# First keys cast in halves, first queries cast and half copied by ScalarE, one key load on another queue, two more warming matmuls

## The chip, the cores and the metric

The kernel runs on one core of a Trainium2 chip. The metric is the device time of one execution in microseconds (us). The core has a matrix engine (PE, TensorE), a vector engine (DVE, VectorE), a scalar engine (ACT, ScalarE), a general one (POOL, GpSimd) and a sequencer that mostly issues transfers (SP, SyncE). Each engine works through its own list of instructions in order, and semaphores hold an instruction back until what it needs is there. Transfers (DMAs) are issued from the lists of SP, ACT and POOL and run beside the engines.

## What is computed

Grouped-query attention: 8 batches, 512 positions, 32 query heads, 8 key/value heads of 64 elements; four query heads share one key/value head.

```python
def reference(Q, K, V):          # Q (8, 512, 32, 64); K, V (8, 512, 8, 64)
    heads_per_group = 32 // 8
    scale = 1.0 / np.sqrt(64)
    K_expanded = np.repeat(K, heads_per_group, axis=2)
    V_expanded = np.repeat(V, heads_per_group, axis=2)
    ...
    scores = np.einsum('bhqd,bhkd->bhqk', Q, K_expanded) * scale
    weights = np.exp(scores - np.max(scores, axis=-1, keepdims=True))
    weights = weights / (np.sum(weights, axis=-1, keepdims=True) + 1e-10)
    output = np.einsum('bhqk,bhkd->bhqd', weights, V_expanded)
    return output.transpose(0, 2, 1, 3).astype(np.float32)
```

## The kernel before

The work is cut into 64 jobs, one for each batch and key/value head; two neighbouring heads make a unit (`u`, with `g` 0 or 1 in it). A job has four query heads in two pairs. For each pair and each of four blocks of 128 keys, PE multiplies keys by queries (`scores`, L217) for both heads of the pair into a PSUM tile of 128 x 2 x 512 numbers. ACT takes the exponential of most of these tiles (`act_tile`, L233), 128 x 1024 at a time; two or three halves per job are instead computed by DVE and POOL from integer arithmetic (`exp_d`, L243, and the functions after it). PE then multiplies the weights by V with a column of ones beside it (`pv`, L300), and DVE divides by the sums (`norm`, L343). The maximum is not subtracted; a flag computed at the end decides whether a general path has to run instead.

The order of the instructions is written out by hand in `fast_path` and no planner moves anything: what stands earlier in the program comes earlier in its engine's list. The job loop (L446) interleaves one job's scores with the last job's products.

The change is in what stands ahead of the loop (L414 to L443). It has these steps.

- Loads. SP's queue gets the first key head in fp32 (`kf[0]`, by `key_head(0)`) and behind it the second (`kf[1]`, `key_head(1)`); ACT's queue gets the first two query heads in fp32 (`qf`, L418). All others go through POOL's queue, which casts to bf16 on the way: the second pair of the first group (`load_q(0, 2, 4)`), the second group's four heads (`load_q(0, 4, 8)`), and then V and K in pieces. POOL also sets a column of ones in the two V tiles (L425).
- Warming. Four matmuls of 128 x 512 zeros (L438) into a scores tile, which nothing reads.
- Keys. `first_keys(0, ...)` (L151): DVE casts `kf[0]` to bf16 into `twice`, each head's 64 columns written two times side by side (L153); PE transposes the four 128-row blocks (L158) into a PSUM bank; `copy()` is DVE's copy of them to `kt_first` (L159).
- Queries. DVE casts `qf` into `qn[0]` (L442). `trans_q(0, bank[:, 0, :], 0, 1)` (L178) lets PE transpose four blocks (L185), and DVE copies the 512 columns to `qt` (L189).

In the loop's job 0, the first scores tile follows, then the transposes of the second pair (`trans_q(0, bank[:, 1, :], 1, NPAIR)`, L470), the second tile, two score products for DVE in the `d_ps` tile, two more tiles, and then twelve transposes: eight of the next job's queries, and four in `first_keys(1, ...)` (L499), whose cast of `kf[1]` stands there on DVE's list. The scores tiles are taken in turn from two PSUM buffers, so the fourth tile waits until the second exponential has been computed.

POOL loads later units of Q only after a gate (L455) that reads the fourth exponential of job 0.

Of the kernel before, what the change touches and what calls it, by code (L numbers as in the profile page):

```python
# [12 lines left out]
BF16 = mybir.dt.bfloat16  # L13
# [3 lines left out]
I32 = mybir.dt.int32  # L17
ALU = mybir.AluOpType
EXP = mybir.ActivationFunctionType.Exp
AX = mybir.AxisListType  # L20


# [17 lines left out]
@with_exitstack  # L40
def kernel(
    ctx: ExitStack,
    tc: tile.TileContext,
    Q: bass.AP,
    K: bass.AP,
    V: bass.AP,
    out: bass.AP,
):
    nc = tc.nc
    flag_pool = ctx.enter_context(tc.tile_pool(name="flag", bufs=1))  # L50
    flag = flag_pool.tile([1, 1], I32, name="flag")
    with ExitStack() as fast, tc.manual_schedule():
        fast_path(fast, tc, Q, K, V, out, flag)
    good = nc.values_load(flag, min_val=0, max_val=128)
    with tc.If(good < 128):
        general_path(tc, Q, K, V, out)


def fast_path(ctx, tc, Q, K, V, out, flag):
    nc = tc.nc  # L60
    B, S, H, D = Q.shape
    KV = K.shape[2]
    HPG = H // KV
    SC = S // 128
    GP = KV // 2
    NU = B * GP
    NPAIR = HPG // 2
# [5 lines left out]
    const_pool = ctx.enter_context(tc.tile_pool(name="const", bufs=1))  # L73
    qnat_pool = ctx.enter_context(tc.tile_pool(name="qnat", bufs=4))
    knat_pool = ctx.enter_context(tc.tile_pool(name="knat", bufs=2))
    qt_pool = ctx.enter_context(tc.tile_pool(name="qt", bufs=3))
# [11 lines left out]
    ident = const_pool.tile([128, 128], BF16, name="ident")  # L88
# [4 lines left out]
    warm = const_pool.tile([128, S], BF16, name="warm")  # L93
# [4 lines left out]
    kf = [const_pool.tile([128, SC, D], FP32, name=f"kf{g}") for g in range(2)]  # L98
    qf = const_pool.tile([128, SC, 2, D], FP32, name="qf")

    kn, qn, kt, qt = {}, {}, {}, {}

    def load_k(b, lo=0, hi=KV):
        if b not in kn:
# [29 lines left out]
    def d_tile():  # L134
        return d_pool.tile([128, 2, S], FP32, name="d_ps")
# [3 lines left out]
    def first_k(gp, swap, bank):  # L139
# [8 lines left out]
                nc.tensor.transpose(ps[:, sc, :], kn[0][:, sc, h:h + 2, :], ident)  # L148
        return lambda: nc.vector.tensor_copy(out=kt_first[:, gp, swap, :], in_=half_bank)

    def first_keys(g, bank):  # L151
        twice = const_pool.tile([128, SC, 2, D], BF16, name=f"twice{g}")
        nc.vector.tensor_copy(  # L153
            out=twice, in_=kf[g][:, :, None, :].to_broadcast((128, SC, 2, D))
        )
        half_bank = bank.bitcast(BF16)[:, 0:S]
        for sc in range(SC):
            nc.tensor.transpose(half_bank[:, sc * 128:(sc + 1) * 128], twice[:, sc, :, :], ident)  # L158
        return lambda: nc.vector.tensor_copy(out=kt_first[:, 0, g, :], in_=half_bank)  # L159

    def dma_k(b):
# [9 lines left out]
    def apart(this, other):  # L171
        if other is not None:
            tc.declare_no_dep(
                this.ins, other.ins, reason="the two are in different banks of one tile"
            )
        return this

    def trans_q(j, bank, lo=0, hi=NPAIR, other=None):  # L178
        u, g = divmod(j, 2)
        ps = bank.bitcast(BF16).rearrange("p (i sc c) -> p i sc c", i=NPAIR, sc=SC)  # L180
        for i in range(lo, hi):
            for sc in range(SC):
                h = g * HPG + 2 * i
                apart(
                    nc.tensor.transpose(ps[:, i, sc, :], qn[u][:, sc, h:h + 2, :], ident), other  # L185
                )
        if u not in qt:
            qt[u] = qt_pool.tile([128, 2, NPAIR, S], BF16, name="qt")
        return lambda: apart(nc.vector.tensor_copy(  # L189
            out=qt[u][:, g, lo:hi, :], in_=ps[:, lo:hi, :, :].rearrange("p i sc c -> p i (sc c)")  # L190
        ), other)

    def check_v(b, sc):
        n = b * SC + sc
        nc.vector.tensor_reduce(  # L195
            out=okv[:, n:n + 1], in_=vt[b % 2][:, sc, :, 0:D], op=ALU.max, axis=AX.XY,
            apply_absolute_value=True,
# [35 lines left out]
    def act_tile(j, n, spare=None):  # L233
# [3 lines left out]
        for _, _, m in group:  # L237
            scores(j, ps[:, m, :], i, kc, m)
        return nc.scalar.activation(  # L239
            out=jobs[j]["pt"][:, i, kc, lo:, :], in_=ps[:, lo:, :], func=EXP, scale=scale  # L240
        )
# [101 lines left out]
    def norm(j, i):  # L343
        st = jobs[j]
        u, g = divmod(j, 2)
        sums = st["pv"][i]
        if u not in osb:
            osb[u] = osb_pool.tile([128, SC, 2 * HPG, D], FP32, name="o_sb")
        p = j * NPAIR + i
        left = NJOB * NPAIR - p  # L350
        k, n = divmod(p, SPB)
        if left <= NLAST:
            inv = inv_last[:, NLAST - left]
        else:
            if k not in invs:
                invs[k] = inv_pool.tile([128, SPB, 2, SC], FP32, name="inv")
            inv = invs[k][:, n]
        nc.vector.reciprocal(out=inv, in_=sums[:, :, :, D:D + 1])  # L358
        if left == 1:
            last_check()  # L360
        h = g * HPG + 2 * i
        nc.vector.tensor_tensor(  # L362
            out=osb[u][:, :, h:h + 2, :].rearrange("p qc m d -> p m qc d"),
            in0=sums[:, :, :, 0:D],
            in1=inv[:, :, :, None].to_broadcast((128, 2, SC, D)),
            op=ALU.mult,
        )
        if u == NU - 1:
            store(u, h, h + 2)
        elif g == 1 and i == NPAIR - 1:  # L370
            store(u, 0, 2 * HPG)
        if left > NLAST and n == SPB - 1:
            full.append((k, SPB))
        if left == NLAST + 1:
            full.append((k, n + 1))
            check_sums()
            vmax = const_pool.tile([128, 1], FP32, name="vmax")
            nc.vector.tensor_reduce(out=vmax, in_=okv, op=ALU.max, axis=AX.X)
            okmin = const_pool.tile([128, 1], FP32, name="okmin")
            nc.vector.tensor_reduce(out=okmin, in_=ok, op=ALU.min, axis=AX.X)  # L380
            nc.vector.scalar_tensor_tensor(
                out=okall, in0=vmax, scalar=V_HI, in1=okmin, op0=ALU.is_le, op1=ALU.mult
            )
# [24 lines left out]
    def pv_tile():  # L408
        return pv_pool.tile([128, 2, S], FP32, name="pv")

    def s_tile():
        return s_pool.tile([128, 2, S], FP32, name="s_ps")

    def key_head(g):  # L414
        nc.sync.dma_start(out=kf[g], in_=K[0, :, g, :].rearrange("(sc p) d -> p sc d", p=128))

    key_head(0)
    nc.scalar.dma_start(out=qf, in_=Q[0, :, 0:2, :].rearrange("(sc p) h d -> p sc h d", p=128))  # L418
    key_head(1)
    make_identity(nc, ident)  # L420
    load_q(0, 2, 4)
    load_q(0, 4, 8)
# [9 lines left out]
    nc.gpsimd.memset(ok, 1.0)  # L432


    nc.vector.memset(warm, 0.0)
    bank = s_tile()
    for j in range(4):
        nc.tensor.matmul(bank[:, 1, :], warm[:, 0:128], warm, start=True, stop=True)  # L438
    copy = first_keys(0, d_tile()[:, 0, :])
    copy()  # L440
    bank = pv_tile()
    nc.vector.tensor_copy(out=qn[0][:, :, 0:2, :], in_=qf)  # L442
    trans_q(0, bank[:, 0, :], 0, 1)()  # L443


    for j in range(NJOB):  # L446
# [3 lines left out]
        u, g = divmod(j, 2)  # L450
# [39 lines left out]
        if not end:  # L490
            bank = d_tile() if j else pv_tile()
            beside = act_tile(j, 4, bank) if taken(j) > 2 else None

            ahead = (j + 1,) if j < 6 else (7, 8) if j == 6 else (j + 2,)
            for n, to in enumerate(ahead):
                if to < NJOB:
                    reads.append(trans_q(to, bank[:, n, :], other=beside))
            if j == 0:
                reads.append(first_keys(1, bank[:, 1, :]))  # L499
            elif j == 1:  # L500
                reads.append(first_k(1, 1, bank[:, 1, :]))
            elif j > 1 and b == 0 and gp + 1 < GP:
                reads.append(first_k(gp + 1, g, bank[:, 1, :]))
        else:
            pv(j, 0, 0, 16)
# [26 lines left out]
        if end:  # L532
# [3 lines left out]
            norm(j, 1)  # L536
    nc.vector.tensor_reduce(out=flag, in_=ends[0], op=ALU.min, axis=AX.X)


def general_path(tc, Q, K, V, out):  # L540
# [8 lines left out]
    with ExitStack() as ctx:  # L549
# [5 lines left out]
        with tc.For_i(0, B, 1) as b:  # L555
            with tc.For_i(0, KV, 1) as g:
# [14 lines left out]
                with tc.For_i(0, HPG, 1) as i:  # L571
# [13 lines left out]
                    for qc in range(SC):  # L585
                        s_ps = ps.tile([128, S], FP32, name="g_s")
                        nc.tensor.matmul(s_ps, q_t[:, qc, :], k_t, start=True, stop=True)
                        top = sb.tile([128, 1], FP32, name="g_top")
                        nc.vector.tensor_reduce(out=top, in_=s_ps, op=ALU.max, axis=AX.X)
                        less = sb.tile([128, S], FP32, name="g_less")  # L590
# [5 lines left out]
                        total = sb.tile([128, 1], FP32, name="g_sum")  # L596
                        nc.scalar.activation(out=e, in_=less, func=EXP, accum_out=total)
                        inv = sb.tile([128, 1], FP32, name="g_inv")
# [56 lines left out]
```

## Time and profile before

| | |
|---|---|
| time, median of 3 runs | 417.14 us (417.10, 417.14, 418.14) |
| time of the profiled execution | 417.43 us |
| its span, first to last instruction | 415.8 us |
| PE busy | 378.1 us (91%) |
| DVE busy | 342.6 us (82%) |
| ACT busy | 400.6 us (96%) |
| POOL busy | 301.5 us (73%) |
| bytes moved by DMA | 67.20 MB, mean 162 GB/s |

Busy shares are means over the whole span. PE's times are partly modelled, since matmuls are pipelined; when one row holds several instructions ("x4"), its time runs from the first one's start to the last one's end. Where the text gives a "chain of waits", it is followed back from the last instruction of the span or of a stretch of it: at each step to what ended the wait, or to the instruction before on the same engine. A row of the order of time has the start in us, the length in us, the engine, the line, the operation, what is written from what, and how many; in square brackets stands the idle time ahead and what ended it.

### The profile page before, as it was taken

The page shows a single profiled execution, that of the slowest core. Times are in us where ns is not written, and L with a number is a line of the kernel's source. Part 1 is how long each engine was busy: PE and PEld are TensorE (multiplying, and loading weights), DVE is VectorE, ACT ScalarE, POOL GpSimd, SP SyncE. Part 2 cuts the span into 40 slices and gives each one's busy share as a digit, 9 for nine tenths or more (in the row PEclk, how much of TensorE's full clock was granted, in tenths as well). Part 3 has the DMA queues.
Part 4 walks back from the last instruction along what each step waited for, and adds up shares of the span by engine and source line. Part 5 has one row for each costly group of instructions (what it writes and reads, how often), then busy time and mean ns, then how long its engine had stood idle before and what let it go on. Part 6 is the DMA issues. An engine that isn't in the chain of part 4 may idle for free.

```text
span 415.8 us, 13054 instructions
## 1 busy us (share of the span) xinstructions
PE 378.1 (91%) x5681; PEld 233.7 (56%) x5681; DVE 342.6 (82%) x609; ACT 400.6 (96%) x449; POOL 301.5 (73%) x213
## 2 busy tenths in 40 slices
PE   5899999999999999999999999999999999999983
PEld 2555655555655555655655655555655555655652
DVE  3677888888888888988888888888889888898875
ACT  3999999999999999999999999999999999999992
POOL 9677665887678886797776897587876887667550
PEclk9999999999999999999999999999999999999998
DMA  9999976799849997399974999669995899732223
GB/s 136 162 165 188 191 154 153 107 214 187 171 139 205 127 222 160 114 217 130 240 181 94 208 180 215 159 85 219 188 173 151 173 160 213 162 110 102 102 102 107
DMA packets 91966, 67.20 MB, mean 162 GB/s; under 512 B 52097, under 2 KB 75137, under 8 KB 91905
## 3 DMA queue, kind: packets, MB, share of 16 engines
q0 software_dynamic: 55488, 24.91, 51.8%
q1 hardware_dynamic: 35888, 41.16, 36.1%
q8 instruction: 45, 0.74, 0.7%
q10 hardware_dynamic: 528, 0.26, 0.2%
q14 instruction: 17, 0.13, 0.1%
HBM read 50.33 MB, written 33.55 MB: 202 GB/s over the span
## 4 chain that ended last, share of the span: by engine, by line
ACT 84%; PE 10%; DVE 3%; issue 1%; DMA 1%; ACTq 0%; DVEq 0%
ACT pt L239 84%; PE s_ps L221 6%; PE pv L315 3%; DMA kf<-in_K_dram 1%; DVE o_sb L362 1%; DVE pt L284 1%; PE pv L185 1%; PE d_ps L185 1%; DVE qt L189 0%; DVE ok L326 0%; ACTq L239 0%; DVE w L267 0%; DVE f L271 0%; PE d_ps L146 0%; DVE twice L153 0%
## 5 line engine op out<-in xcount | busy, mean ns | idle before, releaser
L239 ACT ACTIVATE pt<-s_ps 128x1024 f16<-128x1024 f32 x420 | 397.4, 1289 | 6.1 <-PE s_ps L221 6.1
L315 PEld LDWEIGHTS <-pt 128*128 128x128 f16 x4096 | 142.1, 98 | 75.7 <-issue 56.1
L315 PE MATMUL pv<-v,pt 128*128 128x65 bf16 x4032 | 178.2, 195 | 1.0 <-DVE o_sb L362 0.5
L267 POOL TENSOR_TENSOR w<-g,f 128x1024 bf16<-128x1024 bf16 (+1 forms) x63 | 161.0, 2555 | 5.2
L221 PE MATMUL s_ps<-qt,kt 64*128 64x512 bf16 x728 | 142.6, 383 | 22.3 <-ACT pt L239 16.3
L263 POOL TENSOR_SCALAR g<-f 128x1024 bf16<-128x1024 int16 (+1 forms) x63 | 77.4, 1229 | 96.6 <-DVE f L271 96.6
L250 DVE TENSOR_SCALAR u<-d_ps 128x1024 int16<-128x1024 f32 (+1 forms) x92 | 96.8, 1052 | 1.1 <-PE d_ps L221 1.1
L362 DVE TENSOR_TENSOR o_sb<-pv,inv 128x512 f32<-128x512 f32 x125 | 86.4, 691 | 4.3
L221 PEld LDWEIGHTS <-kt 64*128 64x128 bf16 x896 | 51.8, 93 | 62.3 <-issue 34.9
L358 DVE RECIPROCAL inv<-pv 128x8 f32<-128x8 f32 x125 | 25.9, 207 | 54.6 <-PE pv L315 54.5
L284 DVE TENSOR_TENSOR pt<-u,w 128x1536 uint16<-128x1536 int16 (+1 forms) x64 | 51.1, 798 | 0.1
L221 PE MATMUL d_ps<-qt,kt 64*128 64x512 bf16 x168 | 43.0, 375 | 0.0
L189 DVE COPY qt<-d_ps 128x1024 bf16<-128x1024 bf16 x62 | 42.3, 684 | 0.0
L185 PEld LDWEIGHTS <-q_nat 128*128 128x128 bf16 x512 | 29.3, 99 | 21.1 <-issue 20.0
L185 PE MATMUL d_ps<-ident,q_nat 128*128 128x128 bf16 x496 | 38.3, 220 | 0.0
L271 DVE TENSOR_SCALAR f<-u 128x1536 int16<-128x1536 int16 (+1 forms) x64 | 30.6, 478 | 0.0
L114 POOL DMA_DIRECT2D v<-in_V_dram x32 | 29.0, 909 | 0.1
L129 POOL DMA_DIRECT2D q_nat<-in_Q_dram x33 | 27.0, 818 | 0.2 <-issue 0.2
L221 PE MATMUL s_ps<-qt,kt_first 64*128 64x512 bf16 x112 | 23.1, 407 | 4.2 <-ACT pt L239 3.0
L239 ACT ACTIVATE pt<-d_ps 128x512 f16<-128x512 f32 x28 | 25.2, 899 | 0.0
L195 DVE TENSOR_REDUCE okv<-v 128x1 f32<-128x512 bf16 x32 | 21.6, 676 | 0.0
L221 PEld LDWEIGHTS <-kt_first 64*128 64x128 bf16 x128 | 7.9, 95 | 11.9 <-issue 8.3
(52 smaller groups left out, 44.5 us busy)
## 6 DMA issues: line engine op xcount, KB each, us to landing
out_dram<-o_sb SPq DMA_DIRECT2D x31, 1024.0 KB, 6.8
q_nat<-in_Q_dram POOLq DMA_DIRECT2D x31, 512.0 KB, 6.2
k_nat<-in_K_dram POOLq DMA_DIRECT2D x7, 512.0 KB, 8.3
v<-in_V_dram POOLq DMA_DIRECT2D x28, 128.0 KB, 7.5
kt<-kt SPq DMA_DIRECT2D x14, 256.0 KB, 4.6
out_dram<-o_sb SPq DMA_DIRECT2D x4, 256.0 KB, 2.4
kt<-k_nat SPq DMA_TRANSPOSE x28, 5.8
v<-in_V_dram POOLq DMA_DIRECT2D x4, 96.0 KB, 8.4
```

The lines of the kernel that those rows point to most:

```text
L114: nc.gpsimd.dma_start(out=vt[b % 2][:, sc, lo:hi, 0:D], in_=V[b, sc * 128:(sc + 1) * 128, lo:hi, :],)
L185: nc.tensor.transpose(ps[:, i, sc, :], qn[u][:, sc, h:h + 2, :], ident), other
L189: return lambda: apart(nc.vector.tensor_copy(out=qt[u][:, g, lo:hi, :], in_=ps[:, lo:hi, :, :].rearrange("p i sc c -> p i (sc c)")), other)
L221: return nc.tensor.matmul(ps, keys[64 * m:64 * m + 64, g if u == 0 else g ^ m, kc * 128:(kc + 1) * 128], qt[u][64 * m:64 * m + 64, g, i, : ...
L239: return nc.scalar.activation(out=jobs[j]["pt"][:, i, kc, lo:, :], in_=ps[:, lo:, :], func=EXP, scale=scale)
L250: return lambda: nc.vector.tensor_scalar(out=st["u"][:, lo:hi, :], in0=ps[:, 0:hi - lo, :], scalar1=A_U, scalar2=B_U, op0=ALU.mult, op1=AL ...
L263: engine.tensor_scalar(out=g, in0=f, scalar1=-EXP_F1, scalar2=EXP_K * 2.0 ** (24 * as_bits), op0=ALU.add, op1=ALU.mult,)
L267: engine.tensor_tensor(out=w, in0=g, in1=f.bitcast(FP16) if as_bits else f, op=ALU.mult)
L271: nc.vector.tensor_single_scalar(out=st["f"], in_=st["u"], scalar=1023, op=ALU.bitwise_and)
L284: nc.vector.tensor_tensor(out=st["pt"][:, DPAIR, :, :, :].rearrange("p kc m q -> p (kc m) q")[:, 0:n, :].bitcast(U16), in0=st["u"], in1=st ...
L315: nc.tensor.matmul(st["pv"][i][:, m, qc, :], st["pt"][:, i, kc, m, qc * 128:(qc + 1) * 128], vt[b % 2][:, kc, 2 * gp + g, :], start=(n < 2 ...
L362: nc.vector.tensor_tensor(out=osb[u][:, :, h:h + 2, :].rearrange("p qc m d -> p m qc d"), in0=sums[:, :, :, 0:D], in1=inv[:, :, :, None].t ...
```

## The change

The first keys' cast to bf16 moves out of `first_keys` into a function of its own, `two_keys`, that can do it in pieces; the first key head is cast in two halves (two blocks of 128 rows each), the second in one piece and at another place of the program: after the first queries' copies, not in the loop. The second key head's load is issued from ACT's queue behind the queries' load. The first queries are cast to bf16 by two ACT instructions of two blocks each (the function `Copy`) instead of one DVE instruction. Their four transposes go to two PSUM banks, two to each; DVE copies one bank to `qt`, ACT the other. Warming is four matmuls of 512 columns and one of 256, and one more of 256 columns stands behind the queries' transposes.

```diff
+    def two_keys(g, cuts):
+        twice[g] = const_pool.tile([128, SC, 2, D], BF16, name=f"twice{g}")
+        for lo, hi in zip(cuts[:-1], cuts[1:]):
+            nc.vector.tensor_copy(
+                out=twice[g][:, lo:hi, :, :],
+                in_=kf[g][:, lo:hi, None, :].to_broadcast((128, hi - lo, 2, D)),
+            )
+
     def first_keys(g, bank):
-        twice = const_pool.tile([128, SC, 2, D], BF16, name=f"twice{g}")
-        nc.vector.tensor_copy(
-            out=twice, in_=kf[g][:, :, None, :].to_broadcast((128, SC, 2, D))
-        )
...
-    key_head(0)
+    key_head(0, nc.sync)
     nc.scalar.dma_start(out=qf, in_=Q[0, :, 0:2, :].rearrange("(sc p) h d -> p sc h d", p=128))
-    key_head(1)
+    key_head(1, nc.scalar)
...
+    def keep_busy(*columns):
+        for n in columns:
+            nc.tensor.matmul(spare[:, 1, 0:n], warm[:, 0:128], warm[:, 0:n], start=True, stop=True)
+
     nc.vector.memset(warm, 0.0)
-    bank = s_tile()
-    for j in range(4):
-        nc.tensor.matmul(bank[:, 1, :], warm[:, 0:128], warm, start=True, stop=True)
+    spare = s_tile()
+    keep_busy(S, S, S, S, S // 2)
+    two_keys(0, (0, SC // 2, SC))
     copy = first_keys(0, d_tile()[:, 0, :])
+    for n in range(2):
+        part = slice(n * SC // 2, (n + 1) * SC // 2)
+        nc.scalar.activation(out=qn[0][:, part, 0:2, :], in_=qf[:, part, :, :], func=COPY)
     copy()
     bank = pv_tile()
-    nc.vector.tensor_copy(out=qn[0][:, :, 0:2, :], in_=qf)
-    trans_q(0, bank[:, 0, :], 0, 1)()
+    qt[0] = qt_pool.tile([128, 2, NPAIR, S], BF16, name="qt")
+    halves = [bank[:, n, :].bitcast(BF16)[:, 0:S // 2] for n in range(2)]
+    for sc in range(SC):
+        n, at = divmod(sc, SC // 2)
+        nc.tensor.transpose(
+            halves[n][:, at * 128:(at + 1) * 128], qn[0][:, sc, 0:2, :], ident
+        )
+    keep_busy(S // 2)
+    left = nc.vector.tensor_copy(out=qt[0][:, 0, 0, 0:S // 2], in_=halves[0])
+    apart(nc.scalar.activation(out=qt[0][:, 0, 0, S // 2:], in_=halves[1], func=COPY), left)
+    two_keys(1, (0, SC))
```

More of the change, by code (lines that the diff above doesn't have):

```diff
@@ L19 @@
 EXP = mybir.ActivationFunctionType.Exp
+COPY = mybir.ActivationFunctionType.Copy
 AX = mybir.AxisListType
@@ L99, in fast_path @@
     qf = const_pool.tile([128, SC, 2, D], FP32, name="qf")
-    kn, qn, kt, qt = {}, {}, {}, {}
+    kn, qn, kt, qt, twice = {}, {}, {}, {}, {}
     def load_k(b, lo=0, hi=KV):
@@ L149, in first_k @@
         return lambda: nc.vector.tensor_copy(out=kt_first[:, gp, swap, :], in_=half_bank)
+    def two_keys(g, cuts):
[5 more added lines that the diff above has]
+            )
     def first_keys(g, bank):
-        twice = const_pool.tile([128, SC, 2, D], BF16, name=f"twice{g}")
-        nc.vector.tensor_copy(
-            out=twice, in_=kf[g][:, :, None, :].to_broadcast((128, SC, 2, D))
-        )
         half_bank = bank.bitcast(BF16)[:, 0:S]
         for sc in range(SC):
-            nc.tensor.transpose(half_bank[:, sc * 128:(sc + 1) * 128], twice[:, sc, :, :], ident)
+            nc.tensor.transpose(
+                half_bank[:, sc * 128:(sc + 1) * 128], twice[g][:, sc, :, :], ident
+            )
         return lambda: nc.vector.tensor_copy(out=kt_first[:, 0, g, :], in_=half_bank)
@@ L412, in s_tile, with key_head @@
         return s_pool.tile([128, 2, S], FP32, name="s_ps")
-    def key_head(g):
-        nc.sync.dma_start(out=kf[g], in_=K[0, :, g, :].rearrange("(sc p) d -> p sc d", p=128))
-    key_head(0)
+    def key_head(g, queue):
+        queue.dma_start(out=kf[g], in_=K[0, :, g, :].rearrange("(sc p) d -> p sc d", p=128))
+    key_head(0, nc.sync)
     nc.scalar.dma_start(out=qf, in_=Q[0, :, 0:2, :].rearrange("(sc p) h d -> p sc h d", p=128))
-    key_head(1)
+    key_head(1, nc.scalar)
     make_identity(nc, ident)
@@ L432, in fast_path @@
     nc.gpsimd.memset(ok, 1.0)
+    def keep_busy(*columns):
+        for n in columns:
+            nc.tensor.matmul(spare[:, 1, 0:n], warm[:, 0:128], warm[:, 0:n], start=True, stop=True)
     nc.vector.memset(warm, 0.0)
-    bank = s_tile()
-    for j in range(4):
-        nc.tensor.matmul(bank[:, 1, :], warm[:, 0:128], warm, start=True, stop=True)
+    spare = s_tile()
+    keep_busy(S, S, S, S, S // 2)
+    two_keys(0, (0, SC // 2, SC))
     copy = first_keys(0, d_tile()[:, 0, :])
+    for n in range(2):
+        part = slice(n * SC // 2, (n + 1) * SC // 2)
+        nc.scalar.activation(out=qn[0][:, part, 0:2, :], in_=qf[:, part, :, :], func=COPY)
     copy()
     bank = pv_tile()
-    nc.vector.tensor_copy(out=qn[0][:, :, 0:2, :], in_=qf)
-    trans_q(0, bank[:, 0, :], 0, 1)()
+    qt[0] = qt_pool.tile([128, 2, NPAIR, S], BF16, name="qt")
+    halves = [bank[:, n, :].bitcast(BF16)[:, 0:S // 2] for n in range(2)]
+    for sc in range(SC):
+        n, at = divmod(sc, SC // 2)
+        nc.tensor.transpose(
+            halves[n][:, at * 128:(at + 1) * 128], qn[0][:, sc, 0:2, :], ident
+        )
+    keep_busy(S // 2)
+    left = nc.vector.tensor_copy(out=qt[0][:, 0, 0, 0:S // 2], in_=halves[0])
+    apart(nc.scalar.activation(out=qt[0][:, 0, 0, S // 2:], in_=halves[1], func=COPY), left)
+    two_keys(1, (0, SC))
     for j in range(NJOB):
```

## The prediction

> **What bounds the kernel now.** I read the stretches of the span first, then what ScalarE (ACT) waited for, then the chain of waits over the first 15 us, then the order of time there. The first view gives the busy time of each engine in four stretches (start:end, its length, then PE, weight loads, DVE, ACT, POOL, each with its count).
>
> ```profile
> core 0: us, PE busy (x) PEld busy (x) DVE busy (x) ACT busy (x) POOL busy (x), PEclk, DMA share, GB/s
> 0.00:7.37 7.37, 3.10 (x13) 1.22 (x13) 2.13 (x5) 1.28 (x1) 6.46 (x16) 1.00 0.86 129
> 7.37:12.76 5.39, 5.28 (x30) 2.45 (x30) 2.86 (x5) 3.97 (x4) 4.46 (x7) 1.00 1.38 168
> 12.76:408.10 395.34, 368.47 (x5616) 229.12 (x5613) 334.24 (x591) 395.33 (x444) 290.61 (x191) 1.00 0.89 163
> 408.10:415.80 7.70, 1.25 (x31) 0.92 (x27) 3.38 (x10) 0.00 (x0) 0.00 (x0) 0.78 0.36 107
> ```
>
> From 12.76 to 408.10 us ACT is busy 395.33 of 395.34 us: the exponentials are the bound, and no edit touches them. The change works in the first two stretches alone, so it is worth what it moves the start of that unbroken run. The chain of waits (start us, us, what) says what the start hangs on.
>
> ```profile
> 0.89 3.14 DMA kf<-in_K_dram
> ...
> 4.05 0.69 DVE twice L153
> ...
> 4.78 0.62 PE d_ps L158 x4
> ...
> 5.43 0.42 DVE kt_first L159
> 5.85 0.35 DVE q_nat L442
> ...
> 6.25 0.62 PE pv L185 x4
> ...
> 6.89 0.44 DVE qt L189
> ...
> 7.37 0.61 PE s_ps L221 x2
> 7.98 0.54 PE pv L185 x4
> 8.52 0.56 PE s_ps L221 x2
> ...
> 9.10 1.03 ACT pt L239
> ```
>
> K's load, cast, transposes and copy, then Q's cast, transposes and copy stand in one row up to the first scores at 7.37. Q's load is not in it: it was issued at 0.88 and landed 3.6 us later, 4.49, and waited until 5.77 for DVE. ACT in that time does a table load (1.39 to 2.67) and nothing else. Behind the first scores comes a second part, bound by PE in its order: Q's second pair (7.91), scores 2 (8.45), d_ps scores (9.04), scores 3 (9.42), scores 4 when exponential 2 is done (10.18), twelve transposes (10.72), scores 5 (12.11). ACT starts its first exponential at 8.01 and the second at 9.10, ends the fourth at 12.04, and idles 0.72 us to 12.76.
>
> **The change, in order.** The profiled execution took 417.43 us (span 415.8 and 1.6 around it); the runs' median, 417.14, is 0.29 lower. All times below are on the profiled span.
>
> ```profile
> 4.03 0.41 POOL L425 MEMSET v<- 128x32 bf16 x2
> 4.05 0.68 DVE L153 CAST twice<-kf 128x512 bf16<-128x512 f32 x1 [2.77 <-DMA kf<-in_K_dram]
> ...
> 5.77 0.42 DVE L442 CAST q_nat<-qf 128x512 bf16<-128x512 f32 x1
> ...
> 6.25 0.61 PE L185 MATMUL pv<-ident,q_nat 128*128 128x128 bf16 x4 [0.85 <-DVE q_nat L442]
> ...
> 10.72 1.03 PE L185 MATMUL pv<-ident,q_nat 128*128 128x128 bf16 x8
> ...
> 14.16 0.40 PE L148 MATMUL pv<-ident,k_nat 128*128 128x128 bf16 x4
> ```
>
> *K's cast in halves.* The same cast takes 0.42 us alone and 0.68 beside the two memsets, so 0.26 is waiting, which stays with the first half. No row has half a cast; it lies between 0.21 (all by size) and 0.42 (all fixed). I take 0.30, nearer the first, and the 0.08 by which the next DVE instruction starts ahead of the last one's end: first half done at 4.59, second at 4.81 (bounds 4.73 and 5.05; before 4.73). Two transposes now lie behind it instead of four: the last starts about 0.13 after the second half and takes 0.31, end 5.25 instead of 5.39. K's copy is 5.29 to 5.71. Gain 0.14, bounds +0.2 and -0.1.
>
> [...]
>
> *Q's cast on ACT.* The 0.42 at 5.77 leaves DVE, and Q no longer waits for K. ACT's queue ahead of it has the issues of Q's load and of K group 1's (0.48 each) and the table load: free at 0.88 + 0.96 + 1.28 = 3.1, before Q lands at 4.49. ACT has no cast in this trace. Its exponentials take 1.02 for 1024 columns, and in the steady part (starts at 100.18, 101.09, 101.57 in the order of time) a 1024 one holds 0.91 and a 512 one 0.48, so 0.83 ns a column; 256 columns make 0.38 for one and 0.26 for each behind it. Upper bound: 0.90 each, the 512-column row's mean. I take 0.38 + 0.26: done at 5.15. PE is in order, so Q's transposes follow K's: first two at 5.08, second two at 5.29, last end 5.71. They no longer wait for any cast.
>
> *The copy of Q in two banks, DVE and ACT.* The row is 0.42 for 512 columns; half is between 0.21 and 0.42. DVE's half ends near 5.95 behind K's copy; ACT's starts at 5.75 and takes 0.38: 6.13. First scores at 6.18 instead of 7.37: **-1.19** (bounds -1.3, and -0.7 with both ACT casts at 0.90 and DVE's halves at 0.42).
>
> *K group 1's load on ACT's queue.* It leaves SP's queue, where nothing follows until the first store, and is issued at 1.36 instead of 1.40, behind Q's. Its packets follow Q's; before it landed 3.5 us after issue, about 4.9. Its cast moves ahead of Q's second copy on DVE and lies in DVE's wait near 6 us. It is used by transposes at 9.6 or later, so up to 3 us of lateness are free there; beyond 1.5 us it would hold up Q's second copy behind it on DVE, and so the d_ps scores.
>
> *Warming matmuls.* A fifth, of 256 columns, ends near 3.5, before K lands; the one behind Q's transposes lasts 0.21 while the copies run. Both lie in PE's idle time and cost 0; without that cover they would cost 0.43.
>
> *What is late next.* PE reaches Q's second pair at 6.18 + 0.54 = 6.72. Its load, issued at 1.60 and 5.1 us on its way, lands at 6.7. Transposes at 6.80 instead of 7.91: **-1.11**; the other 0.08 goes into this wait. From there the order repeats earlier: exponential 2 at 7.99, transposes at 9.61 (their load, 2.56 + 6.1 = 8.7, is there), scores 5 at 11.00, exponential 5 at 11.65.
>
> *The 0.72 us hole.* It is PE's. Four transposes take 0.61 us early on and 0.40 at 14.16; four scores 1.04 at 12.11, and two 0.39 at 13.84. The clock column reads 1.00 throughout, so here the rows' spacing tells: PE goes from half to full speed between 12.5 and 13.8. At full speed the twelve transposes save 0.6 and the score pair behind them 0.2; that closes the hole, and exponential 5 then starts 2.85 after exponential 2 (11.95 against 9.10 before): 10.84, **-1.92** in all. Before, full speed came 5.1 to 6.5 us after PE's work became dense at 7.37. Now it is dense, with holes up to 0.3, from 4.63 (first K transpose) or 6.18 (scores): full speed from 9.8 at the earliest to 12.7. The transposes run 9.6 to 10.9. I take half of the further gain, 0.40.
>
> [...]
>
> Sum: 417.43 - 1.11 - 0.40 = 415.9; less 0.29 for the median, 415.6; the hole was maybe smaller in the median runs, so **415.7**. The rest (loads of later units gated by exponential 4, stores, the last 7.7 us) moves along and hides behind ACT.
>
> **Rivals.** (1) *The next load takes the place of the wait.* Q's second pair lands when its slowest DMA engine is done; before it had 1.2 us of room and now none, and K group 1's packets move next to it. For: at the 129 GB/s of the opening 128 KB take 1 us, so most of the 5.1 us is waiting that can vary. Against: the bytes moved in the opening are the same. Each 0.1 us later costs 0.1; 0.5 to 1.1 us later leaves 416.1 to 417.0. (2) *Slower: PE's speed step comes later.* With ACT fed sooner, PE waits for it between 11.5 and 13.5 where before it ran without a hole, and if that thinned stretch keeps it at half speed, the second job meets it. At half speed a job's 16 score pairs (0.43 each), 64 products with V (65 columns: 0.054) and 8 to 12 transposes (128: 0.107) are some 11.3 us against ACT's 6.4: ACT starves 44% of the time. [...] For: one run shown is 1.0 above the others. Against: dense PE work always precedes it. (3) *It does not do what it says:* ACT's casts at the upper bound or the halves held by POOL; the first scores move 0.7 or less: 416.4 to 416.8.
>
> **How the numbers follow.** Forecast 0.62 (own range 414.9 to 416.2), rival 1 0.18, rival 2 0.10, rival 3 0.10. The range 414.9 to 416.9 takes in the closed hole with an early pair (417.14 - 1.92 - 0.3) and most of rivals 1 and 3. A measurement of this kernel tells about 0.3%, 1.25 us: faster means below 415.89. Of the forecast about five sixths lie below it (0.51), of the rivals 0.05: faster 0.56, same 0.37, slower 0.07.
>
> **What would show it.** ACT's first exponential at 6.8 instead of 8.01; Q's casts on ACT from 4.5 and two of them in under 0.7; Q's second pair's transposes at 6.8, with a DMA as what released them; the hole ahead of exponential 5 between 0 and 0.8; ACT unbroken from 10.8 to 11.7 on, for 395.3 us. Wrong if the pair's load lands well after 6.8, if ACT shows holes beyond 13 us, or if the first scores stay near 7.

## The result and the profile after

| | before | changed |
|---|---|---|
| median, 15 runs each | 417.38 us | 416.46 us |
| profiled execution, its span | 417.43, 415.8 us | 416.73, 415.0 us |
| ACT's first exponential | 8.01 us | 7.03 us |
| exponential 5, start of the unbroken run | 12.76 us | 11.78 us |
| end of the last exponential | 408.09 us | 407.14 us |

The ratio of the runs is 0.9979 (95% interval 0.9970 to 0.9987): 0.9 us faster, a small gain that is clear of noise. The 1.4 us forecast were too many. One of the fifteen runs of the kernel before took 453.94 us, for which no trace gives a reason; it is in the median, and the figures below on the spread of the runs leave it out.

The stretches of the span, cut at the first scores, at exponential 5 and at the last exponential's end (start:end, length, then busy PE, weight loads, DVE, ACT, POOL):

```profile
core 0: us, PE busy (x) PEld busy (x) DVE busy (x) ACT busy (x) POOL busy (x), PEclk, DMA share, GB/s
0.00:6.38 6.38, 3.53 (x15) 1.47 (x15) 2.16 (x6) 2.39 (x4) 5.47 (x15) 1.00 0.71 124
6.38:11.78 5.40, 5.32 (x30) 2.46 (x31) 3.11 (x5) 3.99 (x4) 5.31 (x9) 1.00 1.43 169
11.78:407.14 395.36, 368.40 (x5616) 228.98 (x5613) 334.33 (x591) 395.35 (x444) 291.08 (x192) 1.00 0.93 164
407.14:415.00 7.86, 1.26 (x31) 0.92 (x27) 3.38 (x10) 0.00 (x0) 0.00 (x0) 0.76 0.35 105
```

The third stretch is as long as before (395.36 against 395.34) and as full. The second is too (5.40 against 5.39). The whole gain is in the first, 6.38 against 7.37. The chain of waits of the opening shows what it is made of now (start us, us, what):

```profile
0.89 3.09 DMA kf<-in_K_dram
...
4.00 0.61 DVE twice L155
...
4.66 0.39 PE d_ps L163 x2
...
5.09 0.39 PE d_ps L163 x2
5.48 0.44 PE pv L460 x4
...
5.95 0.39 ACT qt L465
...
6.38 0.61 PE s_ps L228 x2
6.99 0.56 PE pv L192 x4
```

Q's cast, 0.42 us of DVE behind K, is gone from the chain, and Q's transposes stand right behind K's. The order of time has the parts (start, length, engine, line, what, and the idle time ahead):

```profile
4.00 1.03 DVE L155 CAST twice<-kf 128x256 bf16<-128x256 f32 x2 [2.73 <-DMA kf<-in_K_dram]
4.04 0.41 POOL L432 MEMSET v<- 128x32 bf16 x2
4.16 0.76 POOL L107 DMA_DIRECT2D k_nat<-in_K_dram  x1
4.46 0.72 ACT L453 ACTIVATE q_nat<-qf 128x256 bf16<-128x256 f32 x2 [1.16 <-DMA qf<-in_Q_dram]
...
6.92 0.61 PE L192 MATMUL pv<-ident,q_nat 128*128 128x128 bf16 x4
...
9.74 1.04 PE L192 MATMUL pv<-ident,q_nat 128*128 128x128 bf16 x8
...
10.56 0.63 PE L163 MATMUL pv<-ident,twice 128*128 128x128 bf16 x4
...
11.78 1.94 ACT L246 ACTIVATE pt<-s_ps 128x1024 f16<-128x1024 f32 x2 [0.65 <-PE s_ps L228]
```

Three things are to be seen. K's cast took 1.03 us in two halves where it took 0.68 whole. ACT's casts took 0.72 for the two, where 0.64 was forecast. And the hole ahead of exponential 5, ACT's idle time between exponentials 4 and 5, is still 0.65 us (0.72 before): the twelve transposes ran at half speed as before, 0.107 us apart. In the span 0.15 more is lost behind the last exponential, of which the last section tells.

### The profile page after: what moved, and what is told of

It reads as the page before. It is cut to its first block, busy times and chain, and to the rows that moved or that the text cites. A ratio compares the mean times of both kernels' runs of the same rounds, so it can differ in the third digit from the quotient of the medians.

```text
span 415.0 us, 13062 instructions
## 1 busy us (share of the span) xinstructions
PE 378.5 (91%) x5683; PEld 233.8 (56%) x5683; DVE 343.0 (83%) x609; ACT 401.7 (97%) x452; POOL 301.9 (73%) x213
## 4 chain that ended last, share of the span: by engine, by line
ACT 74%; PE 15%; DVE 6%; issue 2%; DMA 1%; ACTq 0%; DVEq 0%
ACT pt L246 74%; PE s_ps L228 8%; PE pv L322 5%; DVE pt L291 2%; DVE o_sb L369 1%; DVE qt L196 1%; DMA kf<-in_K_dram 1%; DVE u L257 1%; DVE ok L333 1%; PE d_ps L192 1%; DVE f L278 0%; DVE inv L365 0%; PE d_ps L228 0%; PE pv L192 0%; ACTq L246 0%
```

## The experiments

Each kernel was timed beside runs of the kernel before (417.30 to 417.38 us median); times are medians, ratios are to those runs of the kernel before, made from all runs, so they are not the quotients of the medians. The other columns are of one traced execution each. The step to full speed is where the trace's record of the granted clock begins. (The column PEclk reads 1.00 ahead of it too, as it did in the prediction's view, so the spacing of the transposes is the check: 0.107 us ahead of the step, 0.056 behind it.) The hole is ACT's idle time between exponentials 4 and 5.

| kernel | time, us | ratio (interval) | first scores | step | hole | exponential 5 |
|---|---|---|---|---|---|---|
| before | | | 7.37 | 13.05 | 0.72 | 12.76 |
| changed | 416.46 | 0.9979 (0.9970 to 0.9987) | 6.38 | 11.94 | 0.65 | 11.78 |
| K's cast whole | 416.29 | 0.9984 (0.9973 to 0.9994) | 6.30 | 11.82 | 0.65 | 11.70 |
| memsets later | 416.33 | 0.9982 (0.9972 to 0.9992) | 6.10 | 10.54 | 0.31 | 11.17 |
| Q's cast on DVE | 417.90 | 1.0015 (1.0006 to 1.0024) | 7.79 | 13.27 | 0.64 | 13.19 |
| Q's copy whole | 416.35 | 0.9972 (0.9961 to 0.9983) | 6.48 | 10.15 | 0.01 | 11.18 |
| K 1's load on SP | 416.71 | 0.9990 (0.9980 to 1.0000) | 6.37 | 12.30 | 0.64 | 11.77 |
| ACT cast alone | 416.43 | 0.9979 (0.9968 to 0.9990) | 6.34 | 11.08 | 0.50 | 11.52 |
| warming as before | 416.33 | 0.9976 (0.9966 to 0.9986) | 6.39 | 10.68 | 0.24 | 11.37 |
| seven warming | 415.95 | 0.9966 (0.9953 to 0.9978) | 6.38 | 10.41 | 0.11 | 11.25 |
| dense | 415.37 | 0.9959 (0.9943 to 0.9974) | 6.09 | 4.23 | none | 10.49 |
| before, dense | 416.26 | 0.9968 (0.9956 to 0.9980) | 7.16 | 6.11 | 0.25 | 11.62 |
| dense, memsets later | 415.35 | 0.9948 (0.9934 to 0.9962) | 6.37 | 6.31 | none | 10.44 |
| and load first | 415.20 | 0.9946 (0.9933 to 0.9960) | 6.07 | 4.07 | none | 10.13 |

### What carries the gain of the head

Q's cast back on DVE, all else as changed:

```diff
-    for n in range(2):
-        part = slice(n * SC // 2, (n + 1) * SC // 2)
-        nc.scalar.activation(out=qn[0][:, part, 0:2, :], in_=qf[:, part, :, :], func=COPY)
     copy()
     bank = pv_tile()
+    nc.vector.tensor_copy(out=qn[0][:, :, 0:2, :], in_=qf)
```

> The changed kernel with the first queries' cast on DVE again, in one piece behind the copy of K, and everything else as changed. Theory A (the whole gain of the head is that Q no longer waits for DVE behind K): the cast at 5.9 to 6.3, Q's transposes at 6.33, ACT's half copy until 7.4, first scores near 7.4 as in the kernel before (7.37) and 1.0 later than in the changed one; the time is 0.9 to 1.1 us above the changed kernel's, so 417.2 to 417.5. Rival B (the halved cast, the halved copy and the moved load carry a good part): first scores by 6.9 and the time 0.5 us or less above the changed kernel's.

And that cast on ACT as the only edit to the kernel before:

```diff
+    for n in range(2):
+        part = slice(n * SC // 2, (n + 1) * SC // 2)
+        nc.scalar.activation(out=qn[0][:, part, 0:2, :], in_=qf[:, part, :, :], func=COPY)
     copy()
     bank = pv_tile()
-    nc.vector.tensor_copy(out=qn[0][:, :, 0:2, :], in_=qf)
```

> The kernel before with one part of the change alone: the first queries' cast by two ACT instructions instead of one on DVE. Theory A (this part is the gain of the head; halved cast, halved copy, moved load and added warming are worth nothing on the path): Q's transposes stand right behind K's and end near 5.8, DVE's copies follow one another, the first scores start at 6.3 to 6.4 and the time is the changed kernel's, 416.2 to 416.6. Rival B (the parts need each other): first scores at 6.7 or later, the time 416.8 or more.

Order of time of that kernel:

```profile
4.65 0.72 ACT L443 ACTIVATE q_nat<-qf 128x256 bf16<-128x256 f32 x2 [1.98 <-DMA qf<-in_Q_dram]
...
5.18 0.64 PE L186 MATMUL pv<-ident,q_nat 128*128 128x128 bf16 x4
...
6.34 0.61 PE L222 MATMUL s_ps<-qt,kt_first 64*128 64x512 bf16 x2 [0.52 <-DVE qt L190]
```

Alone it gives the change's whole time: 416.43 against 416.46, first scores at 6.34 against 6.38. Without it the rest of the change is slower than the kernel before, ratio 1.0015, first scores at 7.79. That is 0.4 later than theory A had, and the time is 0.4 above its 417.2 to 417.5. The order of time of that run says why:

```profile
5.87 0.79 DVE L453 CAST q_nat<-qf 128x512 bf16<-128x512 f32 x1
6.71 0.61 PE L458 MATMUL pv<-ident,q_nat 128*128 128x128 bf16 x4 [1.22 <-DVE q_nat L453]
```

The cast that took 0.42 in the kernel before took 0.79 here; the next experiment has the reason. So the move to ACT is the gain, and it also takes that cast off an engine on which it was held up by 0.37 in that run.

### The halved cast, the halved copy and the moved load

```diff
-    two_keys(0, (0, SC // 2, SC))
+    two_keys(0, (0, SC))
```

> The changed kernel with the first keys' cast in one piece again. Theory A (the two halves both wait for POOL's two memsets of V's ones at 4.04 to 4.45: 1.03 us for the two, against 0.68 for the whole cast before): one cast ends near 4.67 instead of 5.03, the last K transpose near 5.34 instead of 5.48, the first scores start near 6.2 instead of 6.38, and exponential 5 near 11.6 instead of 11.78; the time is 0.15 us below the changed kernel's. Rival B (halving gains, since only two transposes stand behind the second half): the first scores start at 6.4 or later and the time is the same or 0.1 us up.

```diff
     load_v_head(0, 0)
+    load_k(0, 2, 4)
     for j in range(2):
         nc.gpsimd.memset(vt[j][:, :, :, D:D + 1], 1.0)
-    load_k(0, 2, 4)
```

> The changed kernel with POOL's two memsets of V's ones one transfer later on its list (behind the issue of K's second group instead of ahead of it). Theory A: with no memset beside them the halves take 0.3 us each; the second ends near 4.55 instead of 5.03, the first scores start near 6.1 to 6.2, limited then by Q's cast on ACT (done near 5.2), exponential 5 near 11.55; 0.2 us below the changed kernel. Rival B (what POOL does beside the casts is any work, the writing of descriptors too, which now starts at 4.04): the halves still end near 5.0 and the first scores stay at 6.4.

With the cast whole, first scores start 0.08 sooner, though K landed 0.14 later in that execution (4.11 against 3.98); a start near 6.2 was expected, 6.30 was measured. With the memsets later both halves are free, and first scores move by 0.28 to 6.10. (Exponential 5 moves by more, to 11.17, as the step came at 10.54 in that execution.) The order of time on DVE and POOL, memsets later:

```profile
4.01 0.50 DVE L155 CAST twice<-kf 128x256 bf16<-128x256 f32 x2 [2.73 <-DMA kf<-in_K_dram]
4.03 0.77 POOL L107 DMA_DIRECT2D k_nat<-in_K_dram  x1
```

0.50 us for both against 1.03. But theory A is only half of it. In the changed kernel the first half ran from 4.00 to 4.60, that is, it ended one free half's length behind the end of the first memset, 4.30. The second ran from 4.52 to 5.03, and the memsets had ended at 4.45. What stood beside it was POOL's issue of a transfer (`load_k(0, 2, 4)`), begun at 4.16. All 14 traces together show a pattern. The table has seven of their casts; the others fit it, apart from those that the memsets held. "Held" is a cast's time less that of a free one, 0.29 for a half and 0.42 for a whole cast; the last column is when the hold ended, counted from the issue's begin. K group 1 is the cast of `kf[1]`.

| cast from fp32 on DVE | POOL's issue began | held for | free, after the issue's begin |
|---|---|---|---|
| memsets later, half 2, at 4.22 | 0.18 before | 0.00 | |
| memsets later, K group 1, at 5.88 | 0.23 before | 0.00 | |
| Q's cast on DVE, at 5.87 | 0.24 before | 0.37 | 0.61 |
| dense, memsets later, half 2, at 4.32 | 0.28 before | 0.30 | 0.58 |
| changed, half 2, at 4.52 | 0.36 before | 0.22 | 0.58 |
| changed, K group 1, at 6.15 | 0.53 before | 0.08 | 0.61 |
| load first, K group 1, at 5.84 | 0.59 before | 0.00 | |

In these traces a cast that started 0.24 to 0.54 us into the issue of one of POOL's transfers waited until some 0.6 us into it (0.7 for the later V loads); one that started up to 0.23 or from 0.59 on did not wait. With the memsets gone, POOL's issue began at 4.03 and the second half had started before the bad stretch, at 4.22. So the memsets held the first half, and the issue of a transfer the second: rival B had that half. It also explains Q's cast on DVE above. That POOL's issue is what holds the cast is read from when the holds begin and end; no run took the issue away altogether. The time's medians here differ by 0.1 to 0.2, less than the intervals; the traces tell these runs apart, the times don't.

```diff
-    halves = [bank[:, n, :].bitcast(BF16)[:, 0:S // 2] for n in range(2)]
...
-    left = nc.vector.tensor_copy(out=qt[0][:, 0, 0, 0:S // 2], in_=halves[0])
-    apart(nc.scalar.activation(out=qt[0][:, 0, 0, S // 2:], in_=halves[1], func=COPY), left)
+    nc.vector.tensor_copy(out=qt[0][:, 0, 0, :], in_=whole)
```

> The changed kernel with the copy of the first queries to qt by DVE alone, 512 columns from one bank. Theory A (ACT's half takes 0.38 us where the whole takes 0.42 on DVE, and DVE is free in time): the copy runs from 5.95 to 6.37 and the first scores start near 6.42 instead of 6.38; the time is the same within 0.2 us. Rival B (the split is worth the half that it takes off DVE): first scores 0.15 later or more.

First scores start 0.05 us behind DVE's copy (6.43), as they do behind ACT's half in the changed kernel (6.33). The copy itself ran 0.42 against 0.38, and it started 0.06 later, as Q landed 0.33 later in this execution. The split is worth 0.04 us.

```diff
-    key_head(1, nc.scalar)
+    key_head(1, nc.sync)
```

> The changed kernel with K group 1's load on SP's queue again, behind group 0's. Theory A (the move takes nothing off the path: both loads landed at 4.9 in before and after, Q's at 4.4 to 4.5): the same first scores, 6.3 to 6.4, and the same time within 0.2 us. Rival B (it let Q's load land sooner): Q lands at 4.6 or later, and the first scores move with it by 0.1 us or more.

Q landed at 4.54 against 4.44, but so did K (4.10 against 3.98), and first scores and exponential 5 are where they were (6.37, 11.77). The time is 0.25 us up with overlapping intervals; the trace gives no reason for it, so the load's effect on time is open, and on the path it is nothing.

### The hole ahead of exponential 5

The warming as it was, and longer:

```diff
-    keep_busy(S, S, S, S, S // 2)
+    keep_busy(S, S, S, S)
...
-    keep_busy(S // 2)
```

> The changed kernel with before's four warming matmuls and none behind Q's transposes. Theory A (the added 512 columns do nothing that can be seen, since full speed came only between 11.5 and 12.9 with them): the same start of exponential 5, 11.7 to 11.9, and the same time within 0.2 us. Rival B (they hold the step where it is): without them full speed comes later than 13 us, job 1's products run at half speed, ACT shows holes behind exponential 7, and the time is 0.4 us or more above the changed kernel's.

```diff
-    keep_busy(S, S, S, S, S // 2)
+    keep_busy(*[S] * 7)
```

> The changed kernel with seven warming matmuls of 512 columns ahead of the keys instead of four and a half, so that PE is at work without a hole from 1.33 to 4.5 us. Theory A (the hole of 0.65 us ahead of exponential 5 is PE at half speed, and the step to full speed comes some time after PE's work becomes dense): full speed before the twelve transposes at 9.7, these then take 0.056 each instead of 0.107, the hole closes, exponential 5 starts near 11.0 instead of 11.78, and the time is 0.6 to 0.9 us below the changed kernel's. Rival B (matmuls of zeros, or of the opening at all, don't bring the step forward): the step stays near 12, the hole at 0.65, the time the same.

Neither theory held in either run, but for the time in the first (416.33, within 0.2 of the changed kernel's). With the old warming the step came sooner than with the new one (10.68 against 11.94), and exponential 5 with it; with seven it came at 10.41, not before 9.7. The hole follows the step, and the step followed neither edit. But the traces fit a rule. The record of full speed lasts 399.359 us in before and in after, 402.773 in "dense, memsets later", 406.186 in "dense": steps of 3.413, and 399.359 is 117.0 of them. So in these traces the clock changes on a grid of 3.413 us, which lies differently to each execution's start. The table counts how much of the stretch that ends at the step PE streamed (a matmul counted with 0.833 ns a column, 0.427 for 512, the spacing of the early ones; pairs side by side once), and of the stretch ahead of it, which did not bring the step, for eight of the 14 traces.

| kernel | filled, stretch that ends at the step | the stretch ahead of it |
|---|---|---|
| before | 0.80 | 0.66 |
| changed | 0.86 | 0.72 |
| K's cast whole | 0.86 | 0.72 |
| K 1's load on SP | 0.76 | 0.72 |
| Q's copy whole | 0.76 | 0.36 |
| seven warming | 0.79 | 0.65 |
| dense | 0.85 | none |
| before, dense | 0.89 | 0.40 |

In all 14 traces the stretch that brings the step is filled to 0.76 or more, and every one that did not to 0.72 or less. Transposes are in this count. Without them the stretches that brought the step are filled from 0.39 up, and one that did not, in the run with seven warming matmuls, to 0.66, so no line parts them; with them it lies between 0.72 and 0.76. That is a fit to 14 traces by one way of counting, with little room between the two sides; no run changed the transposes alone to test it. The changed kernel's stretch from 5.11 to 8.53 missed it by a little.

That gives a test: fill PE's waits.

```diff
-    keep_busy(S, S, S, S, S // 2)
+    keep_busy(*[S] * 7, S // 2)
...
-    keep_busy(S // 2)
+    keep_busy(S // 2, S)
     left = nc.vector.tensor_copy(out=qt[0][:, 0, 0, 0:S // 2], in_=halves[0])
```

> The changed kernel with PE kept at work wherever it waits in the opening: seven and a half warming matmuls of 512 columns ahead of the keys (to 4.5 us) and one and a half behind Q's transposes (to 6.3). Theory A (the step to full speed comes at the end of a stretch of about 3.4 us in which PE was at work nearly all the time, where such stretches begin differing from run to run; in the changed kernel the traces had it at 10.4 to 11.9): with PE dense from 1.33 us on the step comes by 8.2 whatever the beginnings, the twelve transposes at 9.7 run at 0.056 each, the hole ahead of exponential 5 is closed, exponential 5 starts at 10.8 to 11.0, the time is 415.4 to 415.7 and the runs lie closer together (within 0.8 us) than the changed kernel's 1.5. Rival B (the step is a draw that matmuls of zeros have no part in): the step between 9.5 and 13, a time near 416.3 with the same spread.

The same in the kernel before, with nothing else of the change (its keys' and queries' waits filled):

```diff
-    for j in range(4):
-        nc.tensor.matmul(bank[:, 1, :], warm[:, 0:128], warm, start=True, stop=True)
+    keep_busy(*[S] * 7, S // 2)
     copy = first_keys(0, d_tile()[:, 0, :])
+    keep_busy(S, S)
     copy()
...
-    trans_q(0, bank[:, 0, :], 0, 1)()
+    copy = trans_q(0, bank[:, 0, :], 0, 1)
+    keep_busy(S // 2, S)
+    copy()
```

> The kernel before with PE kept at work in its opening, and nothing else of the change: seven and a half warming matmuls of 512 columns ahead of the keys, two behind K's transposes, one and a half behind Q's. Theory A: first scores at 7.37 as before, the step to full speed by 8.2, no hole ahead of exponential 5, which starts near 11.9 instead of 12.76; the time is 0.6 to 0.9 us below before's, about as much as the whole change brings. Rival B (the step is a draw): the hole at 0.3 to 0.7 and the time within 0.2 us of before's.

In both the step came by 8.2, as theory A has it, at 4.23 and 6.11; the ten kernels whose waits were not all filled have it between 10.15 and 13.27. Order of time, dense:

```profile
7.00 0.40 PE L192 MATMUL pv<-ident,q_nat 128*128 128x128 bf16 x4 [0.51 <-DMA q_nat<-in_Q_dram]
...
7.76 5.61 ACT L246 ACTIVATE pt<-s_ps 128x1024 f16<-128x1024 f32 x6 [0.21 <-PE s_ps L228]
...
9.16 0.62 PE L192 MATMUL pv<-ident,q_nat 128*128 128x128 bf16 x8
...
9.61 0.39 PE L163 MATMUL pv<-ident,twice 128*128 128x128 bf16 x4
```

Eight transposes take 0.62 instead of 1.04, four 0.39 instead of 0.63, and from 7.76 ACT has no hole. Exponential 5 came even sooner than theory A had it, at 10.49 instead of 10.8 to 11.0, as the step did. Six of the seven runs lie within 0.6 us (415.10 to 415.67), but the seventh took 417.02, so the spread of 0.8 that theory A had did not come out; the changed kernel's fifteen lie within 1.5. In the kernel before, filling the waits brings 1.05 us, at least as much as the whole change and more than the 0.6 to 0.9 expected. Not all of theory A holds there: a hole of 0.25 is left. It has another cause, the cast of `kf[1]`, for which the last four transposes wait:

```profile
9.97 0.83 DVE L153 CAST twice<-kf 128x512 bf16<-128x512 f32 x1
...
10.86 0.40 PE L158 MATMUL pv<-ident,twice 128*128 128x128 bf16 x4 [0.33 <-DVE twice L153]
```

The first row of dense shows the prediction's first rival come true once the rest is gone: PE stands 0.51 us for Q's second pair, landed at 6.95. So two more, both parts together and that load ahead of the identity:

> The changed kernel with PE kept at work in its waits (seven and a half warming matmuls, and one and a half behind Q's transposes) and POOL's two memsets of V's ones behind the issue of K's second group. Theory A: the two gains add only as far as Q's second pair lets them: its load lands at 6.3 to 6.9, PE reaches it near 6.3, so that exponential 1 starts near 6.4, exponential 2 near 7.4, and exponential 5 at 10.2 to 10.6; 415.1 to 415.4. Rival B (they add in full): exponential 5 by 10.1 and a time under 415.0.

```diff
-    make_identity(nc, ident)
     load_q(0, 2, 4)
+    make_identity(nc, ident)
```

> The same as the run with both, and the load of Q's second pair issued ahead of the identity matrix on POOL's list, at 0.9 instead of 1.6 us. Theory A (that load is what is late once the rest is gone): it lands 0.5 to 0.7 us sooner, near 5.8, PE no longer waits for it, exponentials 1 to 5 run without a hole from 6.4 on, exponential 5 at 10.0 to 10.1; 414.7 to 415.0. Rival B (its packets wait for the opening's other loads, whenever it is issued): it lands at 6.3 or later as before and nothing changes.

The first gives 415.35 and adds nothing to dense that can be told (in this execution the second half of K's cast was held 0.30 by the issue of a transfer, and scores began at 6.37). The last has the lowest median of all, 415.20, ratio 0.9946 (0.9933 to 0.9960), but with five runs its interval overlaps those of the first and of dense; only the trace tells them apart. The pair landed at 5.67, and ACT then runs without a hole from its first exponential:

```profile
core 0: us, PE busy (x) PEld busy (x) DVE busy (x) ACT busy (x) POOL busy (x), PEclk, DMA share, GB/s
0.00:6.50 6.50, 4.87 (x22) 1.90 (x23) 1.97 (x6) 2.39 (x5) 5.21 (x14) 1.00 0.83 140
6.50:405.50 399.00, 371.17 (x5642) 230.38 (x5641) 336.90 (x594) 399.00 (x448) 296.13 (x200) 1.00 0.91 164
```

Exponential 5 starts at 10.13, 0.36 sooner than with dense and near the 10.0 to 10.1 expected; the time is 0.2 above the 414.7 to 415.0 expected.

## Why the prediction was right, and where it was not

*The whole* came out right in its mechanism and too large in its size. 416.46 lies outside the forecast's own range, 414.9 to 416.2, and only within the wider one, which was drawn to take in the rivals; 416.4 to 416.8 was the price of the third rival. Of the 0.76 us between 415.7 and 416.46, some 0.40 is the hole, 0.13 the terms ahead of it (-0.98 instead of -1.11), and 0.24 the starting point: 417.14 was a median of three runs, and that of fifteen is 417.38.

*The bound* was read rightly: from exponential 5 to the end of the last one, 14 traces have between 395.3 and 395.8 us, whatever the opening does. The time moves with the start of that run.

*Q's cast on ACT* was the gain, and its price was nearly right: 5.18 us done against 5.15, the two 0.72 against 0.64. The slow bound given for the first scores, -0.7 with both casts at 0.90, does not follow from its terms: two such casts from 4.5 on end near 6.2, the copies behind the transposes near 7.1, so it should have been about -0.2. It was not needed.

*K's halves* were mis-sized: a gain of 0.14 was given, and it was a loss of 0.09 (last K transpose at 5.48 against 5.39). (A slip of 0.02 is in its sum too: 4.05, 0.26 and 0.30 end the first half at 4.61, not at 4.59.) The term had the memsets hold the first half, which they did, and left the second free. The second half was held by 0.22 beside POOL's issue of a transfer and ended at 5.03; the hold did not last for the whole issue, but until 0.58 us into an issue of 0.76. All of this came through to the first scores, -0.99 instead of -1.19.

*What is late next* was not yet late: the second pair had landed at 6.49 when PE came to it at 6.92. (Of its load's 16 landings in the kernel before, 14 came by 5.65 and the last two at 6.70 and 6.74; in the changed kernel the last came at 6.49.) The term was -1.11 and exponential 5 moved by -0.98, because the wait before was longer, not because of this load. The load does become the wait when PE is faster, as the dense run shows.

*The hole* is the term that failed most. Half of its gain, 0.40, was put into the sum, and nothing came. The hole is 0.07 shorter, but only because exponentials 3 and 4 moved by 0.91 instead of 0.98; from the first of the twelve transposes to exponential 5 PE took 2.04 us in both kernels. The step did move sooner, by 1.11, but it has to come before the transposes and scores 5 are done, and these transposes ended at 11.2 here, ahead of the step at 11.94; it comes in jumps of 3.413 on a grid that lay differently in each trace. Taking half was a mean over a draw. The changed kernel's stretch from 5.11 to 8.53 fell just short, with its transposes counted. The added warming weighs little in that stretch: 512 columns are 0.43 us, 0.13 of a stretch, and the fullest stretch that did not bring the step in the changed kernel reached 0.72 with it.

*Warming that costs nothing* held: nothing on the path waits for it. *The slower rival*, a step so late that job 1 meets half speed, did not occur in these traces: ACT waited 1.4 us for scores in all behind 7 us, the first scores included, and none of it beyond exponential 5.

## What to carry to other kernels

When one engine is busy to the last 0.1% from some point on, an edit to the opening is worth what it moves that point, and the third digit of such a forecast comes from who else uses the path: look for what runs beside each instruction that is cut in two, POOL's memsets and its issues of transfers among it, since each piece can be held up once more (here the second half of K's cast, by 0.22). Before sizing warming work, count how full PE is in every stretch of 3.413 us of the opening, the grid of these traces, and count transposes in: by this count a stretch filled to 0.72 bought nothing here, and filling the waits bought 1 us in both kernels.

## What the runs showed of the hardware that was not expected

In these 14 traces the clock's step sits on a grid of 3.413 us, and the bar, as counted above, lies between 0.72 and 0.76 of a stretch. In the profiled execution of the kernel before the step came at 13.05, so its whole opening ran at half speed (transposes 0.107 us apart up to 11.9). That runs of one kernel differ by 1.5 us (416.72 to 418.24) would fit a grid that lies differently each time; single runs were not traced, so that is not shown.

One and the same DVE cast of 128x512 from fp32 took from 0.42 to 0.83 us, by where it fell in POOL's issue of a transfer, while DVE's copies of that size out of PSUM took 0.41 to 0.43 each time, one of them begun 0.36 into such an issue (at 6.00, with Q's copy whole), and ACT's casts of half that size 0.40 to 0.42 each time. In "before, dense" that 0.83 (held 0.41) is longer by more than the hole of 0.25 that is left.

The end of the span, behind the last exponential, took 7.63 to 7.70 us in six traces and 7.83 to 7.87 in the other eight, whatever the kernel; the 0.15 us by which the profiled span gained less than the exponentials is this.
